# A two-layer trunk on one core: the dt product with both weight parts and both token parts side by side, the norms' first quarter added in two halves, and attention's last chunk read from its bank

## The chip, the cores and the metric

One core of a Trainium2 chip runs the kernel in one launch. The metric is the device time of an execution in microseconds (us), as the median of several. TensorE (PE in the profile) multiplies; its weight loads are listed apart (PEld). VectorE is DVE, ScalarE is ACT, GpSimd is POOL, SyncE is SP. Each engine runs its instructions in the order in which they stand in its program, and an instruction that waits holds up all that stand behind it on the same engine.

## The reference

256 tokens of 2048 columns pass two layers. Layer 0 has a Mamba-2 mixer, layer 1 has differential attention, and each is followed by a SwiGLU network of width 5632. Every one of the four sub-layers stands between two norms, and all is float32:

```python
for i in range(DEPTH):                      # DEPTH = 2
    h = rmsnorm(x, norm_mix_pre[i])
    m = ssd_mixer(h, ...) if i % 2 == 0 else diff_attention(h, ...)
    x = x + rmsnorm(m, norm_mix_post[i])
    h = rmsnorm(x, norm_ffn_pre[i])
    x = x + rmsnorm(swiglu(h, w_gate, w_up, w_down), norm_ffn_post[i])

# in the mixer: one product u @ w_in gives z, x, B, C and dt (64 columns, one for each head)
dt = softplus(dt + dt_bias);  a = -exp(a_log)
y = ssd_chunked_scan(xs * dt[..., None], dt * a, bm, cm)
```

## The kernel before

**Products.** A float32 product is made of three products of a shorter format (fp32r): weights and tokens are each cut into a high part and the rest (`hi`, `lo`), and TensorE adds hi·hi, hi·lo and lo·hi into one PSUM bank. For the weights `prep` (L126) does it, 512 columns at a time: ACT casts `hi` (L133), DVE subtracts it from the raw tile for `lo` (L134). The tokens lie in four tiles `xT[n]` of shape [128, 4, 2, 256]: for each of 16 blocks of the 2048 columns the high and the low part of all 256 tokens side by side. In the usual product (`mv`, L177) a 128-token block stands still and 512 weight columns move.

**Order.** Blocks of weights are counted by `tick`, and `later(k, fn)` (L155) hangs a piece of work k blocks further on. From this the framework's scheduler writes each engine's order when the program is built. PSUM has 8 banks: 4 for accumulators (`acc`) and 4 for all else (`aux`).

**dt.** The mixer begins with the first z chunk (`z_chunk(0)`), of weight blocks numbered hi0/lo0, hi1/lo1 and so on. Hung into it are the load of dt's 2048x64 weights, their split (`dt_split`, L366: one cast, one subtraction), and `dt_product` (L371): for each of 16 blocks three matmuls, in which the 64 weight columns stand still and 256 tokens move, 48 in all, into 64 partitions of the bank `pdt`. The tokens are not normalised yet. Their row norms come from ACT squares of the rows (`row_stats`, L381), and are spread over all partitions by two matmuls into `pb` (L312) and a DVE copy to `rstd_bc` (L313). `dt_chain` (L416) multiplies `pdt` with it and goes on in some 30 small DVE and ACT instructions on 64 partitions (softplus, the cumulated decay), which the scheduler puts between the subtractions of lo8 to lo16. `dt_token` (L446) transposes the results (`pdt_tok`).

**Norms.** The last product of each sub-layer (`out_proj`, L682) comes in four column chunks n of 512 and two token blocks t. Where a chunk's accumulator is ready, `evac` (L745) moves it to `m[(t, n)]`. For attention, where the product is made in one pass (`first`), that is an ACT copy (L749); for the others DVE adds it to what is there (L751). `sums` (L687) takes the sum of squares on ACT (L302) and multiplies by the norm's weight: POOL for n < 3, DVE into `mw` for n = 3 (L691). After the last chunk `norm_chain` (L645) runs for that t: the mean (`ms_post`, DVE, L90), its power -1/2 (`rs_post`, POOL, L93), four DVE instructions of 512 columns `x = m * rs + x` (L655), and for each of them four 128x128 transposes on TensorE into `ptx` (L661), from which ACT and DVE write the new `xT` (L666, L667). The next sub-layer's weights are then multiplied with these. The chain runs four times: step 0 behind the mixer (about 695 us), step 1 behind the first SwiGLU (1403), step 2 behind attention (1811) and, in a form that ends in the output, at the end. Last blocks of the old product (`ah_`, `al_` are the two parts of its tokens) lie beside the chain of t = 0, first blocks of the next one beside that of t = 1.

Of the kernel before, what the change touches and what calls it, by code (L numbers as in the profile page):

```python
# [16 lines left out]
P = 128  # L17
S = 256
# [23 lines left out]
def trunk_kernel(ctx, tc, x_rows, x_cols, vec_cols, vec64, post_rows, lam_rows,  # L42
# [19 lines left out]
    def aux(name):  # L62
        return auxp.tile([P, 512], F32, tag="aux", name=name)
# [300 lines left out]
        nc.sync.dma_start(dts["raw"], w_dt)  # L364

    def dt_split():  # L366
        dts["hi"] = hlA.tile([P, KD, NH], F32R, tag="hi", name="dthi")
        dts["lo"] = hlA.tile([P, KD, NH], F32R, tag="lo", name="dtlo")
        split(dts["hi"], dts["lo"], dts["raw"])

    def dt_product():  # L371
        pdt = dts["p"] = accp.tile([P, 512], F32, tag="acc", name="pdt")
        for kt in range(KD):
            xh, xl = xT_hi[kt // 4][:, kt % 4], xT_lo[kt // 4][:, kt % 4]
            for q, (w, xx) in enumerate(((dts["hi"], xh), (dts["hi"], xl), (dts["lo"], xh))):
                nc.tensor.matmul(pdt[:NH, :S], w[:, kt], xx, start=(kt == 0 and q == 0),
                                 stop=(kt == KD - 1 and q == 2))

    rs0, rh0 = [], []

# [264 lines left out]
    def norm_chain(t, ss4, last_mw, step, final, t512):  # L645

        rn = rstd_of(ss4[:, 3:4], D, f"post{step}_{t}", ss4[:, 0:1])
        for n in range(4):
            mw = last_mw if n == 3 else m[(t, n)]
            xt = xres[(t, n)]  # L650
            if final and n == 0:
                nc.scalar.activation(mw, mw, AF.Copy, scale=rn)
                nc.gpsimd.tensor_tensor(xt, xt, mw, op=ALU.add)
            else:
                nc.vector.scalar_tensor_tensor(xt, mw, rn, xt, op0=ALU.mult, op1=ALU.add)  # L655
            if final:
                nc.sync.dma_start(out[t * P:(t + 1) * P, n * 512:(n + 1) * 512], xt)
                continue
            pt = aux("ptx")
            for j in range(4):  # L660
                nc.tensor.transpose(pt[:, j * P:(j + 1) * P], xt[:, j * P:(j + 1) * P], ident)  # L661
            for j in range(4):
                sl = slice(t * P, (t + 1) * P)
                sc = pre_cols[step + 1][:, 4 * n + j:4 * n + j + 1]
                pj = pt[:, j * P:(j + 1) * P]
                nc.scalar.activation(xT_hi[n][:, j, sl], pj, AF.Copy, scale=sc)  # L666
                nc.vector.scalar_tensor_tensor(xT_lo[n][:, j, sl], pj, sc, xT_hi[n][:, j, sl].bitcast(F32),  # L667
                                               op0=ALU.mult, op1=ALU.subtract)

        def stats():  # L670
            st = small.tile([P, 4], F32, tag="ss4", name="ss_x", bufs=3)
            for n in range(4):
                row_sumsq(st[:, n:n + 1], xres[(t, n)], t512("junk"))
            s1_ = small.tile([P, 1], F32, tag="ss1", name="ssx", bufs=3)
            nc.vector.tensor_reduce(s1_, st, axis=AX.X, op=ALU.add)
            rstd[(step, t)] = rstd_of(s1_, D, f"pre{step}_{t}")


        if not final:
            later(5, stats)  # L680

    def out_proj(w, first, last, acts, kgs, step, final, lag, t512, pw, scale=None, ns=range(4), two={}, forms=None, md=None, mid=None):  # L682
# [1 line left out]

        def sums(t, n):  # L687
            mt = m[(t, n)]
            row_sumsq(ss4[t][:, n:n + 1], mt, t512("junk"))
            dst = t512("mw") if n == 3 else mt  # L690
            (nc.vector if n == 3 else nc.gpsimd).tensor_tensor(dst, mt, pw(n), op=ALU.mult)  # L691
            return dst
# [7 lines left out]
        def up_stat(i, j, t):  # L700
            return stat(up[i], j, t)

        def row(t, e):
            if t not in ss4:
                ss4[t] = small.tile([P, 4], F32, tag="ss4", name="ss_m", bufs=3)
            if e not in summed[t]:
                summed[t].add(e)
                return sums(t, e)

        ss4 = {}  # L710
        summed = {t: set() for t in range(NT)}
# [25 lines left out]
        for n in ns:  # L737
# [7 lines left out]
            def evac(t, ps, n=n):  # L745
                if first:
                    if n == 0:
                        m_tile(t)
                    nc.scalar.copy(m[(t, n)], ps)  # L749
                else:  # L750
                    nc.vector.tensor_tensor(m[(t, n)], m[(t, n)], ps, op=ALU.add)  # L751
                if not last:
                    return
                for e in range(n):
                    row(t, e)
                dst = row(t, n)
                if n == 2:
                    p3 = small.tile([P, 1], F32, tag="ss1", name="p3", bufs=3)
                    nc.vector.tensor_reduce(p3, ss4[t][:, 0:3], axis=AX.X, op=ALU.add)
                    nc.vector.tensor_scalar(ss4[t][:, 0:1], p3, 1.0 / D, EPS, op0=ALU.mult, op1=ALU.add)  # L760
                if n == 3:
                    norm_chain(t, ss4[t], dst, step, final, t512)
# [5 lines left out]
    for half in range(2):  # L768
        if half == 0:
# [2 lines left out]
            later(5, lambda: (row_stats(1), dt_split()))  # L772
            later(7, halve)
            later(8, dt_product)
            later(8, lambda: later(1, make_rstd_bc(rstd_bc, rs0, lambda: s1.tile([P, P], F32, tag="dg", name="dg"))))
            later(10, dt_chain)
            later(15, dt_token)
# [359 lines left out]
```

## Time and profile before

| | |
|---|---|
| runs | 2540.88, 2540.77, 2540.26 us; median 2540.77 |
| profiled execution | 2539.5 us, of which the span of the profile 2537.7 |
| TensorE clock granted, mean | 0.998 of full speed |
| busy: PE, DVE, ACT, POOL | 2517.8, 1902.6, 1364.7, 222.4 us |
| the chain that ended last | PE 93%, DVE 2%, ACT, issue and DMA 1% each |
| DMA | 536 MB, 211 GB/s on average |

A row of the timeline gives its start, its length, engine, line, operation, what it writes and reads, shape, and how many instructions of one kind it stands for. In brackets is how long the engine had been idle before it, and what it waited for last. Matmuls are pipelined: one of 512 columns is shown with 0.39 us, and the next starts 0.23 us after it.

### The profile page before, as it was taken

Reading aid. Unit: us, or ns where it says so; the run is one execution under the profiler, and the core shown is the slowest. Engines: PE = TensorE matmul, PEld = TensorE weight load, DVE = VectorE, ACT = ScalarE, POOL = GpSimd, SP = SyncE. Lnnn points to the kernel's source line nnn. Section 1 sums busy time; section 2 is a strip of 40 time slices with the busy share of each in tenths; the row PEclk is TensorE's granted clock in tenths of the full one; section 3 lists DMA queues with packets and bytes.
Section 4 is the critical chain, followed back from the end, with each engine's and each line's share of the span. In section 5 each row is a group of like instructions: output and inputs, shape, how many; then the busy total and the mean of one; then the engine's idle time right before and its main releaser. Section 6 shows DMA issues by size and latency. Waiting matters only on the chain.

```text
span 2537.7 us, 31211 instructions
## 1 busy us (share of the span) xinstructions
PE 2517.8 (99%) x11866; PEld 2072.2 (82%) x11866; DVE 1902.6 (75%) x2274; ACT 1364.7 (54%) x1655; POOL 222.4 (9%) x214
## 2 busy tenths in 40 slices
PE   9999999999999999999999999999999999999998
PEld 8877888788888888888888888887888888888886
DVE  6777547777687888977887765566688889878985
ACT  5767556666565454544454654455655454535453
POOL 0111000110110000001001100001100000010002
PEclk9999999999999999999999999999999999999999
DMA  7555555455776776778677544544666966786673
GB/s 287 190 169 182 189 191 198 166 183 177 254 260 210 253 238 210 236 231 243 210 237 246 189 150 166 183 151 156 241 223 201 294 216 208 235 262 213 205 252 146
DMA packets 141366, 536.16 MB, mean 211 GB/s; under 512 B 14176, under 2 KB 30880, under 8 KB 114208
## 3 DMA queue, kind: packets, MB, share of 16 engines
q1 hardware_dynamic: 125584, 502.91, 57.3%
q0 software_dynamic: 15264, 30.94, 6.5%
q8 instruction: 93, 1.52, 0.2%
q14 instruction: 57, 0.47, 0.0%
q10 hardware_dynamic: 368, 0.32, 0.0%
HBM read 516.22 MB, written 17.89 MB: 210 GB/s over the span
## 4 chain that ended last, share of the span: by engine, by line
PE 93%; DVE 2%; ACT 1%; issue 1%; DMA 1%; POOL 0%; SPq 0%; DVEq 0%; ACTq 0%; POOLq 0%
PE acc L238 38%; PE acc L187 34%; PE cp L238 8%; PE acc L212 5%; PE acc L214 2%; DVE lo L134 1%; PE sc L1013 1%; DMA mt<-acum_d 1%; PE pt_f L291 1%; ACT hi L133 1%; PE py L568 1%; PE ptx L661 0%; PE po L1049 0%; PE pc L475 0%; PE pp L1040 0%
## 5 line engine op out<-in xcount | busy, mean ns | idle before, releaser
L134 DVE TENSOR_TENSOR lo<-raw,hi 128x2048 fp32r<-128x2048 f32 (+2 forms) x451 | 848.6, 1888 | 362.4 <-ACT hi L133 353.2
L133 ACT CAST hi<-raw 128x2048 fp32r<-128x2048 f32 (+2 forms) x451 | 699.8, 1557 | 593.9 <-DVE raw L263 195.4
L238 PE MATMUL acc<-hi,xT 128*128 128x512 f32 x1840 | 589.2, 390 | 0.0
L187 PE MATMUL acc<-hi,xT 128*128 128x512 f32 x1792 | 588.9, 399 | 0.0
L238 PEld LDWEIGHTS acc<-hi,xT 128*128 128x128 f32 x1840 | 345.3, 188 | 71.5
L187 PEld LDWEIGHTS acc<-hi,xT 128*128 128x128 f32 x1792 | 335.9, 188 | 73.4 <-issue 4.9
L238 PE MATMUL acc<-lo,xT 128*128 128x512 f32 x920 | 358.1, 389 | 0.0
L187 PE MATMUL acc<-lo,xT 128*128 128x512 f32 x896 | 352.1, 393 | 1.1 <-DVE lo L134 1.1
L133 ACT CAST hi<-rawm 128x2048 fp32r<-128x2048 f32 (+1 forms) x115 | 207.8, 1807 | 173.4 <-DVE rawm L263 108.3
L134 DVE TENSOR_TENSOR lo<-rawm,hi 128x2048 fp32r<-128x2048 f32 (+1 forms) x115 | 248.0, 2157 | 69.9 <-ACT hi L133 66.1
L238 PEld LDWEIGHTS acc<-lo,xT 128*128 128x128 f32 x920 | 172.7, 188 | 35.5
L187 PEld LDWEIGHTS acc<-lo,xT 128*128 128x128 f32 x896 | 169.0, 189 | 38.0 <-DVE lo L134 3.6
L238 PE MATMUL acc<-hi,ah_f 128*128 128x512 f32 x468 | 183.1, 391 | 0.0
L238 PE MATMUL acc<-hi,al_f 128*128 128x512 f32 x468 | 182.1, 389 | 0.0
L238 PE MATMUL acc<-lo,ah_f 128*128 128x512 f32 x468 | 182.1, 389 | 0.0
L212 PE MATMUL acc<-xT,hi 128*128 128x512 f32 x512 | 179.8, 397 | 0.0
L238 PE MATMUL cp<-hi,ff 128*128 128x512 f32 x468 | 156.9, 389 | 0.0
L214 PE MATMUL acc<-xT,lo 128*128 128x256 f32 x512 | 142.6, 280 | 0.0
L138 DVE SCALAR_TENSOR_TENSOR lo<-raw,cols,hi 128x512 fp32r<-128x512 f32 x128 | 92.5, 767 | 57.2 <-ACT hi L137 56.9
L137 ACT ACTIVATE hi<-raw,cols 128x512 fp32r<-128x512 f32 x128 | 84.8, 715 | 58.9 <-PE acc L187 41.4
L212 PEld LDWEIGHTS acc<-xT,hi 128*128 128x128 f32 x512 | 96.1, 188 | 22.6
L238 PEld LDWEIGHTS acc<-hi,al_f 128*128 128x128 f32 x468 | 87.8, 188 | 18.4
(279 smaller groups left out, 3470.4 us busy)
## 6 DMA issues: line engine op xcount, KB each, us to landing
raw<-in_w_zxbc_dram SPq DMA_DIRECT2D x77, 1024.0 KB, 4.8
raw<-in_w_d_dram SPq DMA_DIRECT2D x98, 512.0 KB, 5.9
raw<-in_w_g_dram SPq DMA_DIRECT2D x96, 512.0 KB, 5.9
raw<-in_w_u_dram SPq DMA_DIRECT2D x96, 512.0 KB, 5.8
raw<-in_w_qkv_dram SPq DMA_DIRECT2D x48, 1024.0 KB, 4.8
raw<-in_w_so_dram SPq DMA_DIRECT2D x32, 1024.0 KB, 4.8
rawm<-in_w_g_dram SPq DMA_DIRECT2D x64, 512.0 KB, 5.8
rawm<-in_w_u_dram SPq DMA_DIRECT2D x64, 512.0 KB, 6.0
```

The costliest lines, as they stand in the source:

```text
L133: nc.scalar.copy(hi, raw)
L134: nc.vector.tensor_tensor(lo, raw, hi.bitcast(F32), op=ALU.subtract)
L137: nc.scalar.activation(hi[:, j], raw[:, j], AF.Copy, scale=scale[j])
L138: nc.vector.scalar_tensor_tensor(lo[:, j], raw[:, j], scale[j], hi[:, j].bitcast(F32), op0=ALU.mult, op1=ALU.subtract)
L187: nc.tensor.matmul(acc[t], a, b[:, j], start=(i == 0 and j == 0 and q == 0), stop=(i == last and j == 1 and q == 2))
L212: nc.tensor.matmul(acc[ct], hi[:, j, cs], x.rearrange("p a s -> p (a s)"), start=(i == 0 and j == 0), stop=False)
L214: nc.tensor.matmul(acc[ct][:, :S], lo[:, j, cs], x[:, 0], start=False, stop=(i == last and j == 1))
L238: nc.tensor.matmul(acc[k], a, b, start=first and q == 0, stop=last and q == 2)
L291: nc.tensor.transpose(pt[:, j], src[:, j * P:(j + 1) * P], ident)
L568: nc.tensor.matmul(py[e * 64:(e + 1) * 64, a], xd[c][:, 2 * a + e], mts[c][:, 2 * a + e], start=True, stop=True)
L1013: nc.tensor.matmul(sc[c][:, h], qT[cp, h % 2, ts], kT[cp, h % 2, :nk * P], start=True, stop=True)
```

## The change

Three places change.

- **dt.** The weights' two parts are written side by side, in two tiles of 8 blocks each, so that one stationary tile holds 64 high and 64 low columns; the 512 moving columns are the 256 high and 256 low token parts. 16 matmuls replace 48. The bank then holds four sums: high weights in partitions 0 to 63, low ones in 64 to 127, each for high and low tokens. `dt_sum` adds them: ACT copies the low tokens' half from the bank (`dta`), DVE adds the high tokens' half (`dtb`), and a matmul with a 128x64 matrix of two stacked identities (`fold`) adds the two halves of the partitions into `pdt2`. low·low is now part of the sum.
- **Norms.** The first of the four additions `x = m * rs + x` is made in two pieces of 256 columns (in the chains of steps 0, 1 and 2).
- **Attention's last chunk.** The fourth chunk isn't copied to `m`: ACT's squares and DVE's product with the norm's weight both read the accumulator's bank.

```diff
     def dt_split():
-        dts["hi"] = hlA.tile([P, KD, NH], F32R, tag="hi", name="dthi")
-        dts["lo"] = hlA.tile([P, KD, NH], F32R, tag="lo", name="dtlo")
-        split(dts["hi"], dts["lo"], dts["raw"])
+        for k in range(2):
+            d = dts[k] = hlA.tile([P, 8, 2, NH], F32R, tag=("hi", "lo")[k], name="dthl")
+            split(d[:, :, 0], d[:, :, 1], dts["raw"][:, 8 * k:8 * k + 8])
 
     def dt_product():
         pdt = dts["p"] = accp.tile([P, 512], F32, tag="acc", name="pdt")
         for kt in range(KD):
-            xh, xl = xT_hi[kt // 4][:, kt % 4], xT_lo[kt // 4][:, kt % 4]
-            for q, (w, xx) in enumerate(((dts["hi"], xh), (dts["hi"], xl), (dts["lo"], xh))):
-                nc.tensor.matmul(pdt[:NH, :S], w[:, kt], xx, start=(kt == 0 and q == 0),
-                                 stop=(kt == KD - 1 and q == 2))
+            nc.tensor.matmul(pdt, dts[kt // 8][:, kt % 8].rearrange("p a h -> p (a h)"),
+                             xT[kt // 4][:, kt % 4].rearrange("p a s -> p (a s)"),
+                             start=kt == 0, stop=kt == KD - 1)
+
+    def dt_sum():
+        a = s1.tile([P, S], F32, tag="v", name="dta", bufs=2)
+        b = s1.tile([P, S], F32, tag="th", name="dtb", bufs=2)
+        nc.scalar.copy(a, dts["p"][:, S:])
+        nc.vector.tensor_tensor(b, dts["p"][:, :S], a, op=ALU.add)
+        fold = s1.tile([P, NH], F32, tag="fold", name="fold", bufs=1)
+        nc.vector.tensor_tensor(fold, ident[:, :NH], ident[:, NH:], op=ALU.add)
+        dts["p"] = aux("pdt2")
+        nc.tensor.matmul(dts["p"][:NH, :S], fold, b, start=True, stop=True)
...
-                nc.vector.scalar_tensor_tensor(xt, mw, rn, xt, op0=ALU.mult, op1=ALU.add)
+                for sl in (slice(0, 256), slice(256, 512)) if n == 0 else (slice(0, 512),):
+                    nc.vector.scalar_tensor_tensor(xt[:, sl], mw[:, sl], rn, xt[:, sl], op0=ALU.mult, op1=ALU.add)
...
-        def sums(t, n):
-            mt = m[(t, n)]
+        def sums(t, n, mt):
...
-                return sums(t, e)
+                return sums(t, e, m[(t, e)] if mt is None else mt)
...
-                    nc.scalar.copy(m[(t, n)], ps)
+                    if not last or n < 3:
+                        nc.scalar.copy(m[(t, n)], ps)
...
-                dst = row(t, n)
+                dst = row(t, n, ps if first and n == 3 else None)
...
             later(8, dt_product)
+            later(9, dt_sum)
```

With other work to place, the scheduler also moves instructions that the diff doesn't name, at the two ends of the engines' programs that follow. Numbers behind a name are those of its buffer, and lines below L369 have another number in the new program (L417 became L429, L655 became L669, L661 became L675).

On TensorE at the end of dt's product, before: `pdt` is dt's bank, `pb` the one with the spread norms, `acc` belongs to the first z chunk.

```order
L376 MATMUL pdt_357<-xT3_102,dthi_285 64x256 x2
L376 MATMUL pdt_357<-xT3_102,dtlo_286 64x256
L312 MATMUL pb_433<-dg_406,ones_103 128x128
L312 MATMUL pb_433<-dg_407,ones_103 128x128
L187 MATMUL acc_171<-hi6_311,xT3_102 128x512
L187 MATMUL acc_196<-hi6_311,xT3_102 128x512
L187 MATMUL acc_171<-lo6_312,xT3_102 128x512
```

The same place after the change:

```order
L376 MATMUL pdt_359<-xT3_102,dthl_288 128x512 x4
L389 MATMUL pdt2_409<-dtb_404,fold_407 64x256
L312 MATMUL pb_411<-dg_376,ones_103 128x128
L312 MATMUL pb_411<-dg_377,ones_103 128x128
L187 MATMUL acc_171<-hi6_313,xT3_102 128x512
L187 MATMUL acc_196<-hi6_313,xT3_102 128x512
L187 MATMUL acc_171<-lo6_314,xT3_102 128x512
```

The `fold` matmul now stands directly behind the product whose sums ACT and DVE have to read before it, and ahead of `pb` and of all of hi6.

On DVE at the same place, before: `lo6` to `lo9` are weight subtractions, `rh0_1` is the last small step of the row norms.

```order
L391 TENSOR_SCALAR rh0_1_283<-rs_in1_281 128x1
L134 TENSOR_TENSOR lo6_312<-raw_309,hi6_311 128x1024
L134 TENSOR_TENSOR lo7_334<-raw_309,hi7_333 128x1024
L313 COPY rstd_bc_105<-pb_433 128x256
L417 TENSOR_TENSOR dtr_163<-pdt_357,rstd_bc_105 64x256
L134 TENSOR_TENSOR lo8_413<-raw_410,hi8_412 128x1024
L134 TENSOR_TENSOR lo9_438<-raw_410,hi9_437 128x1024
```

And after the change:

```order
L403 TENSOR_SCALAR rh0_1_283<-rs_in1_281 128x1
L385 TENSOR_TENSOR dtb_404<-pdt_359,dta_403 128x256
L313 COPY rstd_bc_105<-pb_411 128x256
L134 TENSOR_TENSOR lo6_314<-raw_311,hi6_313 128x1024
L134 TENSOR_TENSOR lo7_336<-raw_311,hi7_335 128x1024
L429 TENSOR_TENSOR dtr_163<-pdt2_409,rstd_bc_105 64x256
L430 TENSOR_SCALAR dtr_163<-dtr_163,v64_157 64x256
L432 SCALAR_TENSOR_TENSOR ta_164<-dtr_163 64x256
L134 TENSOR_TENSOR lo8_383<-raw_380,hi8_382 128x1024
```

The copy of `pb` has moved ahead of lo6 and lo7, behind the new `dtb`; three steps of dt's chain have moved ahead of lo8.

On DVE in the second norm chain behind attention (step 2, t = 1), before: `lo449` and `lo450` belong to the second SwiGLU's gate weights, `ms_post2_1` and `rs_post2_1` are this chain's.

```order
L134 TENSOR_TENSOR lo449_14687<-raw_14684,hi449_14686 128x2048 [waits DMAHW2_49,PE_49]
L691 TENSOR_TENSOR mw_14607<-m_14123,wpost_14359 128x512 [waits Activation_49]
L134 TENSOR_TENSOR lo450_14718<-raw_14715,hi450_14717 128x2048 [waits DMAHW3_49,PE_49,Activation_49]
L90 TENSOR_SCALAR ms_post2_1_14609<-ss_m_14125 128x1 [waits Activation_49]
L655 SCALAR_TENSOR_TENSOR x_11014<-m_14123,rs_post2_1_14611,x_11014 128x512 [waits Pool_49]
```

And after the change:

```order
L704 TENSOR_TENSOR mw_14588<-acc_14411,wpost_14341 128x512 [waits Activation_49]
L90 TENSOR_SCALAR ms_post2_1_14590<-ss_m_14107 128x1
L669 SCALAR_TENSOR_TENSOR x_10994<-m_14105,rs_post2_1_14592,x_10994 128x256 [waits Pool_49]
L669 SCALAR_TENSOR_TENSOR x_10994<-m_14105,rs_post2_1_14592,x_10994 128x256
L669 SCALAR_TENSOR_TENSOR x_10994<-m_14105,rs_post2_1_14592,x_10994 128x512
L669 SCALAR_TENSOR_TENSOR x_10996<-m_14105,rs_post2_1_14592,x_10996 128x512
L681 SCALAR_TENSOR_TENSOR xT0_99<-ptx_14596,cols_91,xT0_99 128x128 [waits Activation_49]
L669 SCALAR_TENSOR_TENSOR x_10996<-m_14105,rs_post2_1_14592,x_10996 128x512 [waits DVE_49]
L134 TENSOR_TENSOR lo450_14700<-raw_14697,hi450_14699 128x2048 [waits DMAHW3_49]
```

lo450 has gone from ahead of the chain to behind all of its additions, and `mw`, which reads the bank, waits for ACT. On TensorE, just ahead of this, the last matmul of attention's product (`acc` from hi446 and `al_o3`) stood directly behind its fellows, ahead of the 11 matmuls with hi448 and lo448; it now stands behind these 11.

## Rows read from the trace of the kernel before

**Rows 1.** The page, part 1: busy us, share, instructions of each engine.
```profile
PE 2517.8 (99%) x11866; PEld 2072.2 (82%) x11866; DVE 1902.6 (75%) x2274; ACT 1364.7 (54%) x1655; POOL 222.4 (9%) x214
```

**Rows 2.** The waits of TensorE: total us, times, longest us.
```profile
PE ptx L661 <- DVE x L655: 1.5, 3, 0.7
PE acc L187 <- DVE lo L134: 1.1, 4, 0.3
```

**Rows 3.** Line L376, dt's matmuls with the high weights: ns, first and last start.
```profile
L376 PE MATMUL pdt<-xT,dthi x32: 276/276/281, 21.8 to 29.8; 128*64 128x256 f32 x32
```

**Rows 4.** Timeline of the end of dt's product, 26 to 32 us: start, length.
```profile
26.67 0.39 PE L376 MATMUL pdt<-xT,dthi 128*64 128x256 f32 x2
...
28.02 2.00 ACT L133 CAST hi<-raw 128x1024 fp32r<-128x1024 f32 x2 [0.62 <-DMA raw<-in_w_zxbc_dram]
...
29.10 2.36 DVE L134 TENSOR_TENSOR lo<-raw,hi 128x1024 fp32r<-128x1024 f32 x2 [0.68 <-ACT hi L133]
...
29.96 0.28 PE L376 MATMUL pdt<-xT,dtlo 128*64 128x256 f32 x1
...
30.08 0.60 PE L312 MATMUL pb<-dg,ones 128*128 128x128 f32 x4
...
30.44 0.70 PE L187 MATMUL acc<-hi,xT 128*128 128x512 f32 x2
...
30.98 0.39 PE L187 MATMUL acc<-lo,xT 128*128 128x512 f32 x1
...
31.21 0.62 PE L187 MATMUL acc<-hi,xT 128*128 128x512 f32 x2
...
31.38 0.42 DVE L313 COPY rstd_bc<-pb 128x256 f32<-128x256 f32 x1
```

**Rows 5.** Windows: PE, PEld, DVE, ACT, POOL busy (instructions), granted clock, DMA.
```profile
44.00:57.00 13.00, 12.86 (x57) 9.68 (x55) 12.37 (x25) 5.55 (x8) 0.00 (x0) 1.00 0.65 230
...
136.00:140.00 4.00, 2.86 (x16) 2.52 (x17) 1.91 (x3) 2.97 (x5) 0.00 (x0) 1.00 0.54 227
```

**Rows 6.** Timeline of step 0's chains (t = 0 at 696, t = 1 at 710).
```profile
696.75 2.08 DVE L655 SCALAR_TENSOR_TENSOR x<-m,rs_post,x 128x512 f32<-128x512 f32 x3 [0.66 <-POOL rs_post L93]
...
709.81 0.50 PE L187 MATMUL acc<-lo,xT 128*128 128x512 f32 x1 [0.27 <-DVE lo L134]
...
710.39 2.28 DVE L134 TENSOR_TENSOR lo<-raw,hi 128x2048 fp32r<-128x2048 f32 x1
...
710.55 2.53 POOL L93 TENSOR_TENSOR rs_post<-ms_post,mhalf 128x1 f32<-128x1 f32 x1 [13.84 <-DVE ms_post L90]
...
713.92 0.66 PE L661 MATMUL ptx<-ident,x 128*128 128x128 f32 x4 [0.23 <-DVE x L655]
```

**Rows 7.** Timeline of step 1's second chain.
```profile
1416.12 2.29 DVE L134 TENSOR_TENSOR lo<-raw,hi 128x2048 fp32r<-128x2048 f32 x1
...
1418.46 0.50 PE L187 MATMUL acc<-lo,xT 128*128 128x512 f32 x1 [0.27 <-DVE lo L134]
```

**Rows 8.** Timeline of step 2's chains (t = 0 at 1811, t = 1 at 1823).
```profile
1811.15 0.59 ACT L749 COPY m<-acc 128x512 f32<-128x512 f32 x1 [2.17 <-PE acc L187]
...
1811.77 0.64 ACT L302 ACTIVATE junk<-m 128x512 f32<-128x512 f32 x1
1811.77 0.69 DVE L691 TENSOR_TENSOR mw<-m,wpost 128x512 f32<-128x512 f32 x1 [0.46 <-ACT m L749]
...
1814.30 0.63 PE L661 MATMUL ptx<-ident,x 128*128 128x128 f32 x4 [0.69 <-DVE x L655]
...
1823.41 0.39 PE L187 MATMUL acc<-hi,al_o 128*128 128x512 f32 x1
...
1824.32 1.92 ACT L133 CAST hi<-raw 128x2048 fp32r<-128x2048 f32 x1
...
1826.27 2.29 DVE L134 TENSOR_TENSOR lo<-raw,hi 128x2048 fp32r<-128x2048 f32 x1
...
1830.16 0.66 PE L661 MATMUL ptx<-ident,x 128*128 128x128 f32 x4
```

More of the change, by code (lines that the diff above doesn't have):

```diff
@@ L701, in up_stat, with row @@
             return stat(up[i], j, t)
-        def row(t, e):
+        def row(t, e, mt=None):
             if t not in ss4:
```

## The prediction, made before the run

> **What bounds the kernel now.** First the page: TensorE is busy for 2517.8 of the 2537.7 us [rows 1], so time can only go where its work becomes less or where it waits. Then its waits, which the reader is to compare with the three edits: at the norms it waits 1.5 us in three places for the first addition `x`, and 1.1 us in four places for a weight subtraction `lo` [rows 2]. Then the timeline at each edited place, for what stands ahead of and behind the wait on ACT and DVE [rows 4, 6 to 8]. A change under 0.2% (5.1 us) can't be told from none with this kernel; the waits that the edits can remove are below that from the start, and what remains is to see which way the small terms add up.
>
> **dt's product.** Removed are 48 matmuls. Two stand in 0.39 us where one is shown with 0.276 [rows 3, 4], so one starts 0.114 us after the other: 48 x 0.114 = 5.45 us. Added are 16 of 512 columns. Such a matmul is followed by the next after 0.23 us (30.98 and 31.21 [rows 4]): 16 x 0.23 = 3.68. The `fold` matmul is plain float32 with 256 moving columns; the nearest row is `pb`, where 0.36 us pass for 4 records of 128 columns [rows 4], so 0.36 for it. In TensorE's work this is 3.68 + 0.36 - 5.45 = -1.4 us.
>
> But the fold stands directly behind the product, with two readers of the bank between them. Before, `pb` started at 30.08; without the fold it would start 1.77 earlier, at 28.31, and the last product matmul would be done about 28.45. ACT's copy of 256 columns I price by DVE's copy of the same shape, 0.42 [rows 4], so 28.5 to 28.9; `dtb` as much, to 29.4; the fold starts about 29.45. TensorE idles for 1.1 us, `pb` follows at 29.8, hi6 at 30.2. So far 0.25 us are left of the gain (30.44 before [rows 4]). ACT casts hi6 only behind the copy, 28.9 to 29.9, in time for that.
>
> Next is DVE. Before, lo6 started at 29.10, and `rstd_bc` stood behind lo7 [rows 4]. Now `dtb` and `rstd_bc` stand ahead of lo6, and `rstd_bc` waits for `pb`: 30.4 to 30.8. lo6 runs from 30.85 for 1.18 (half of the pair's 2.36) to 32.05. The matmul that waits for it stood at 30.98 and comes 1.07 later, with 1.4 us of new idle time ahead of it. Here the saving is gone and TensorE is late.
>
> What of it remains is set some 25 us later, where TensorE transposes the ends of dt's chain. DVE, which makes this chain between its subtractions, has little slack: it is busy for 12.37 of 13.00 us from 44 to 57 us [rows 5]. It lost 1.33 us (lo6 from 29.10 to 30.85, less the 0.42 of `rstd_bc` that it has now done), and 0.63 of slack can take that up, so the chain ends about 0.6 late, and TensorE with it, whatever it saved in matmuls. **Term: +0.6**, from -1.4 (DVE has more slack before 44 than I think and the waits vanish) to +1.1. The split in two pieces casts as many columns, and its first piece is ready sooner; I cost it at nothing, since dt's first product matmuls have z matmuls beside them; without that cover the start of one more instruction on each engine, about 0.1.
>
> **The halved addition.** An addition of 512 columns takes 0.69 (2.08 for three [rows 6]); one of 256 I take at 0.42, by the nearest row of that width (`rstd_bc` [rows 4]). The first two transposes may start some 0.3 earlier; the second half has to be ready behind two transposes and a matmul, and is. In the chains of t = 0 TensorE waits 0.7 for this (1814.30 [rows 8], longest in [rows 2]). But in the new order one matmul that stood ahead of the transposes now stands behind the first two, so that TensorE comes 0.23 earlier to the wait: of 0.3 about 0.1 is gained. Three chains: **-0.2** (0 to -0.9).
>
> Its chains of t = 1 depend on what DVE does between. Step 0: the wait for a `lo` at 709.81, and the power `rs_post` at 710.55, which took 2.53 us beside the subtraction at 710.39 [rows 6], where DVE waits only 0.66 for it at 696.75 [rows 6]. The new order puts that subtraction ahead of the mean, and nothing but the additions behind it: one wait on `lo` goes (0.4 by starts), a smaller one on the next comes (0.3), five matmuls more lie ahead of the transposes at 713.92, whose wait of 0.4 by starts goes on paper. **-0.5** (-0.8 to +0.3). Step 1: the subtraction that started at 1416.12, on which the matmul at 1418.46 already waited [rows 7], now stands behind two small DVE steps which need ACT, and ACT is then loading a function table. It comes about 0.8 later and its successor 0.5, against 0.7 of waits that go: **+0.6** (-0.5 to +1.3).
>
> **The bank read directly.** It removes ACT's copy, 0.59, from the chain [rows 8]. In its place, the squares (0.64, with their sum read out some 0.8) begin at the copy's time. Before, `mw` (0.69) ran beside the squares, both at 1811.77 [rows 8]; now both read one bank, and DVE's instruction waits for ACT's. So the mean is ready after 0.8 + 0.7 instead of 0.6 + 0.8: at t = 0 it is no earlier than before (+0.1), **0**, with -0.6 as the far end.
>
> The Trainium skill, "PSUM — Partial Sum Buffer", section "PSUM bank collisions raise a hardware error", says that two engines may not be in one bank at the same time, two reads included, so that software has to order them. No row of before has two readers at once, and the new program holds the wait. If that rule and the wait were not there, both of step 2's chains would gain about 0.6, and the time would come to 2541.9 in place of the forecast.
>
> At t = 1 the order moved more. The last matmul into the bank stood at 1823.41 [rows 8], and now stands 11 matmuls later: 1823.41 + 11 x 0.23 = 1825.9, ready at 1826.3. From there: squares to 1827.15, `mw` to 1827.9, mean to 1828.1, power 0.6 to 1828.7, half an addition to 1829.1, transposes at 1829.2. They stood at 1830.16 [rows 8], but with the matmuls that TensorE has meanwhile: after the moved one 10 stand ahead of them, so it is free at 1828.4 and waits 0.8, where it had waited 0.2. ACT's cast of hi450 started at 1824.32 [rows 8] and is now behind the squares, 1827.2 to 1829.1. lo450, at 1826.27 before [rows 8], stands behind all additions: 1831.6 to 1833.9. TensorE comes to it at about 1832.7: 1.2 of new wait. **+1.8** (-0.1 to +2.5; below zero if the squares' bank is ready earlier than I count).
>
> Queues: on SP a few weight loads changed places, and on POOL one power with an accumulating DMA; the weights are two loads ahead there, which hides it. Behind 1836 us nothing moves. No instruction is cut or added elsewhere.
>
> **Sum.** 0.6 - 0.2 - 0.5 + 0.6 + 0 + 1.8 = +2.3 us. The profiled execution took 2539.5 (span 2537.7 and 1.8 around it), the median of the runs is 1.3 above it: 2539.5 + 2.3 + 1.3 = 2543.1, so **2543 us**, within 0.2% of before.
>
> **Rivals.**
> 1. *The removed work pays.* dt's -1.4 stays because DVE catches up before TensorE transposes the chain; halves and bank read gain their far ends at t = 0, and t = 1 costs nothing. For it: all the waits named are DVE's or ACT's, and before 44 us ACT waits often. Against: DVE at 12.37 of 13.00 [rows 5]. -1.4 - 0.9 - 0.5 - 0.6 = -3.4: 2537.4 us. Even this is within 0.2%.
> 2. *lo450 holds up what stands behind it* (the slower side). Its 2.29 us [rows 8] now lie on DVE between the additions and the subtractions that make the next tokens' low parts. If TensorE needs these as soon as lo450, it waits the 2.29 once more on top of the 1.2, and step 2 costs 4.1 in place of 1.8. It decides from the point where TensorE's first matmul with the new low parts stands less than 2.3 us behind its first with lo450. For it: the additions of t = 1 end at 1831.6, one subtraction behind another. Against: the weights of hi449 to hi451 with t = 0 are work that TensorE still has. 2545.4 us; with dt's upper end as well 2545.9, with step 1's 2546.6.
> 3. *A lowered clock.* The two new pauses of 1.1 and 1.4 lie within 4 us. Were the granted clock to fall from 2.4 to 1.2 GHz for those 4 us, they would take 4 us more: 2547 us. Against: behind the longest wait of the kernel, in the stretch from 136 to 140 where TensorE is busy for 2.86 of 4.00, it stands at 1.00 [rows 5].
> 4. *Nothing moves:* the scheduler's changes and the edits cancel at each place, 2540 to 2541 us. For it: the sum's terms are each smaller than their ranges.
>
> **Chances.** Forecast (2541.5 to 2544.5) 0.47; rival 4 0.2; rival 1 0.17; rival 2 0.12; rival 3 0.04. The range of 8 in 10 leaves out rival 3, the last part of rival 2 and the lower part of rival 1: 2537.5 to 2546. Faster by over 0.2% would be below 2535.7, beyond even rival 1, and is left for what I overlook: 0.06. Slower by over 0.2% is above 2545.9: rival 3, half of rival 2 and a little of the forecast's upper end, 0.12. The same: 0.82.
>
> **What would show it.** On the page after: TensorE's instructions fall, its busy time hardly. dt right: a matmul of line 389 starts about 1.1 us after the product, a matmul with lo6 waits about 1.4 us for DVE, and the first matmuls of hi16 stand 0.3 to 0.9 later than before; wrong, if hi16 is earlier than before. The bank read right: `mw` starts when the squares end, 0.8 after them, at both t; wrong, if they overlap. Step 2 right: a matmul waits some 1.2 us for lo450; wrong, if lo450 is there in time. The halves: transposes of two, not four, ahead of the next matmul, the wait ahead of them 0.1 shorter at t = 0. The whole is wrong if TensorE's waits in the three chains together fall by more than 1 us, or if a place that I hold for unmoved, behind 1836 us, differs.

## The result, and the profile after

The changed kernel takes 2544.31 us (median of 22 executions, 2542.29 to 2545.37), the kernel before beside it 2539.91 (22, 2539.15 to 2541.11): 4.4 us more, ratio 1.0016 with a 95% interval of 1.0010 to 1.0023. The profiled execution took 2543.73 us, of which the span 2542.0.

TensorE's work hardly changed on the page (2517.8 us in [rows 1]), so the loss is waits:

```profile
PE 2517.2 (99%) x11836; PEld 2070.8 (81%) x11836; DVE 1904.8 (75%) x2283; ACT 1363.5 (54%) x1655; POOL 219.7 (9%) x214
```

The waits of TensorE after the change (total us, times, longest), to be laid beside [rows 2]:

```profile
PE acc L187 <- DVE lo L134: 3.8, 4, 1.2
PE ptx L675 <- DVE x L669: 2.1, 5, 0.6
...
PE pdt L389 <- DVE dtb L385: 0.9, 1, 0.9
...
PE cp L238 <- DVE lo L134: 0.3, 1, 0.3
PE py L580 <- ACT mt L523: 0.2, 1, 0.2
```

The wait for a weight subtraction `lo` has risen from 1.1 to 3.8 us in as many places, and the one for the new `dtb` is added; the two small ones at the end are not among the waits of before. Where they came is read by following one matmul through both traces: counted in order on its line, the same matmul starts so much later after the change:

| landmark (time before) | later by, us | what lies between |
|---|---|---|
| 20 us | 0.15 | start |
| 31.4, dt's end | 1.49 | fold and lo6 |
| 62 | 1.24 | dt's chain |
| 690 | 1.61 | no edited place |
| 709 | 1.42 | step 0, t = 0 |
| 735 | 1.00 | step 0, t = 1 |
| 1395 | 1.31 | no edited place |
| 1436 | 2.17 | step 1 |
| 1812 | 2.82 | no edited place |
| 1822 | 2.51 | step 2, t = 0 |
| 1838 | 4.24 | step 2, t = 1 |
| 2525 | 4.23 | no edited place |

So dt costs about 1.2 (0.15 of it from the start on), step 0 gives 0.6, step 1 costs 0.9, step 2 gives 0.3 and then costs 1.7: 2.9 us at the edited places. The other 1.3 are hops, places between the edited ones at which the lateness grows by up to 0.3 us. Two of them, 0.30 at 124 us and 0.24 at 1018, are the two small waits above. The experiments show what the hops are worth.

**dt.** The timeline of the changed kernel from 28 to 33 us, the counterpart of [rows 4]:

```profile
28.55 0.37 ACT L384 COPY dta<-pdt 128x256 f32<-128x256 f32 x1 [0.71 <-PE pdt L376]
...
28.82 3.98 ACT L133 CAST hi<-raw 128x1024 fp32r<-128x1024 f32 x4
28.95 0.43 DVE L385 TENSOR_TENSOR dtb<-pdt,dta 128x256 f32<-128x256 f32 x1
29.43 0.65 PE L389 MATMUL pdt<-dtb,fold 128*64 128x256 f32 x2 [0.92 <-DVE dtb L385]
...
30.47 0.71 PE L187 MATMUL acc<-hi,xT 128*128 128x512 f32 x2
30.76 0.42 DVE L313 COPY rstd_bc<-pb 128x256 f32<-128x256 f32 x1 [1.38 <-PE pb L312]
31.10 2.35 DVE L134 TENSOR_TENSOR lo<-raw,hi 128x1024 fp32r<-128x1024 f32 x2
32.37 0.50 PE L187 MATMUL acc<-lo,xT 128*128 128x512 f32 x1 [1.18 <-DVE lo L134]
```

hi6's first matmul stands where it stood (30.47 for 30.44): what the shorter product saved went into the wait for the fold. DVE sat idle for 1.38 us until `pb` was there, then copied it, and only then made lo6, whose matmul comes at 32.37 in place of 30.98. Behind that TensorE gets hardly any of it back: from 44 to 57 us it was busy for 12.86 of 13.00 us before [rows 5], and is so throughout after the change (busy PE, PEld, DVE, ACT, POOL; granted clock, DMA):

```profile
44.00:57.00 13.00, 13.00 (x58) 10.24 (x57) 12.21 (x25) 5.75 (x7) 0.00 (x0) 1.00 0.73 244
```

**Norms.** Step 0's second chain, the counterpart of [rows 6]:

```profile
711.40 2.28 DVE L134 TENSOR_TENSOR lo<-raw,hi 128x2048 fp32r<-128x2048 f32 x1
...
714.49 0.55 POOL L93 TENSOR_TENSOR rs_post<-ms_post,mhalf 128x1 f32<-128x1 f32 x1 [16.17 <-DVE ms_post L90]
...
715.61 0.44 PE L675 MATMUL ptx<-ident,x 128*128 128x128 f32 x2 [0.22 <-DVE x L669]
```

The power takes 0.55 where it took 2.53, as no subtraction lies beside it now. In step 1 the subtraction on which [rows 7] already waited comes later:

```profile
1418.29 2.29 DVE L134 TENSOR_TENSOR lo<-raw,hi 128x2048 fp32r<-128x2048 f32 x1
...
1420.62 0.50 PE L187 MATMUL acc<-lo,xT 128*128 128x512 f32 x1 [1.06 <-DVE lo L134]
```

It started at 1416.12 before; of the 2.17 between, 1.37 are the lateness that TensorE already had, 0.80 are new.

**Step 2**, both chains, the counterpart of [rows 8]:

```profile
1813.97 0.60 ACT L302 ACTIVATE junk<-acc 128x512 f32<-128x512 f32 x1 [2.17 <-PE acc L187]
...
1814.69 0.69 DVE L704 TENSOR_TENSOR mw<-acc,wpost 128x512 f32<-128x512 f32 x1 [0.56 <-ACT junk L302]
...
1816.80 0.41 PE L675 MATMUL ptx<-ident,x 128*128 128x128 f32 x2 [0.59 <-DVE x L669]
...
1828.41 0.39 PE L187 MATMUL acc<-hi,al_o 128*128 128x512 f32 x1
...
1828.84 0.60 ACT L302 ACTIVATE junk<-acc 128x512 f32<-128x512 f32 x1 [2.48 <-PE acc L187]
...
1829.42 1.90 ACT L133 CAST hi<-raw 128x2048 fp32r<-128x2048 f32 x1
...
1829.56 0.69 DVE L704 TENSOR_TENSOR mw<-acc,wpost 128x512 f32<-128x512 f32 x1 [1.13 <-ACT junk L302]
...
1831.58 0.44 PE L675 MATMUL ptx<-ident,x 128*128 128x128 f32 x2 [0.51 <-DVE x L669]
...
1834.08 2.28 DVE L134 TENSOR_TENSOR lo<-raw,hi 128x2048 fp32r<-128x2048 f32 x1
...
1836.42 0.50 PE L187 MATMUL acc<-lo,xT 128*128 128x512 f32 x1 [1.00 <-DVE lo L134]
```

The squares begin where the copy began (1811.15 + 2.82), `mw` begins 0.72 after them, where both began together before. At t = 1 the last al_o matmul stands at 1828.41 (1823.41 before: 2.5 by the lateness, 2.5 by the 11 matmuls), and lo450 is ready 1.0 us after TensorE wants it.

### The profile page after: what moved, and what is told of

Same layout as the page of the kernel before. It is cut to its first block, busy times and chain, and to the rows that moved or that the text cites. A ratio compares the mean times of both kernels' runs of the same rounds, so it can differ in the third digit from the quotient of the medians.

```text
span 2542.0 us, 31156 instructions
## 1 busy us (share of the span) xinstructions
PE 2517.2 (99%) x11836; PEld 2070.8 (81%) x11836; DVE 1904.8 (75%) x2283; ACT 1363.5 (54%) x1655; POOL 219.7 (9%) x214
## 4 chain that ended last, share of the span: by engine, by line
PE 93%; DVE 2%; ACT 2%; issue 1%; DMA 1%; POOL 0%; SPq 0%; DVEq 0%; ACTq 0%; POOLq 0%
PE acc L238 38%; PE acc L187 34%; PE cp L238 8%; PE acc L212 5%; PE acc L214 2%; DVE lo L134 1%; PE sc L1028 1%; ACT hi L133 1%; DMA mt<-acum_d 1%; PE pt_f L291 1%; PE py L580 1%; ACT mt L523 0%; PE po L1064 0%; PE ptx L675 0%; PE pc L487 0%
```

## The experiments

Each was timed beside the kernel before on the same chip, over 11 executions, the last two kernels over one each. The median of before was 2540.28 us for the first four and for the next four, 2540.73 for the two after. The difference given behind each time is the one to that median. Besides, the same matmul is followed through the traces as above.

**dt's part alone** (the hunks of `dt_split`, `dt_product` and `dt_sum`):

```diff
...
+            later(9, dt_sum)
```

> Only the dt part of the change; norms and attention's last chunk as before. Theory: DVE, with dtb and the copy of pb ahead of lo6, and TensorE behind the fold make dt's part about +1.3 us late at lo6 and +1.1 at the first matmuls of hi16, and nothing after that differs: +1.1 us against before in the whole. Rival: the small shifts that the changed kernel's trace shows behind dt (+0.25 near 150 us, +0.3 near 1018, +0.65 between 1490 and 1690) come from the changed order and belong to this part: then this kernel shows them too and the whole is +2 or more.

2543.08 us, +2.8, ratio 1.0010 (1.0001 to 1.0019). In its trace dt costs 1.2 at 62 us, and nothing moves at the norms; hops of 0.2 to 0.3 follow at 124, 152, 1018 and near 1630. The place is as expected, the median is 1.7 us above it. Neither theory is met as a whole, and the rival is met in part: the hops at 124 (0.29 to 0.32) and at 1018 (0.24 to 0.31) stand in all four traces of kernels with dt's part as in the change. In the nine others the first is 0.15 at most and the second absent, so these two go with dt's part and its order; why, is open. Hops at the other places stand in kernels without dt's part too.

**The halved addition alone:**

```diff
+                for sl in (slice(0, 256), slice(256, 512)) if n == 0 else (slice(0, 512),):
```

> Only the halved first addition. My account in the prediction put the loss behind attention (t = 1) down to the bank read. Theory now: it is the halves that make the scheduler put the last al_o matmul 11 matmuls later, and that alone costs the chain. In this kernel lo450 stays ahead of the mean on DVE, behind a cast of hi450 that waits for the late copy: TensorE waits about 2.2 us for lo450, and step 2 is +2.0 in all; step 0 -0.6, step 1 +0.85, so +2.2 us against before. Rival (the bank read is what costs): step 2 here gains 0.3 at t = 0 and loses nothing at t = 1, and the whole is about 0 (-0.6 + 0.85 - 0.3).

2544.50, +4.2, ratio 1.0016 (1.0007 to 1.0025): as much as the whole change. In the trace step 0 -0.66, step 1 +0.85, step 2 -0.24 at t = 0 and +3.98 at t = 1. The rival, which was the account of the prediction, falls: the loss behind attention is there without the bank read. It is larger than expected (3.7 in step 2 for 2.0), though the wait for lo450 is shorter (1.83 for 2.2); the reason is in the clock. Its timeline and a window behind that wait:

```profile
1832.52 0.50 PE L187 MATMUL acc<-lo,xT 128*128 128x512 f32 x1 [1.83 <-DVE lo L134]
```

```profile
1834.00:1836.00 2.00, 2.00 (x9) 1.51 (x8) 2.00 (x5) 0.37 (x1) 0.00 (x0) 0.58 0.86 356
```

The clock granted from 1834 to 1838 is 0.57 to 0.58: TensorE has fallen mostly to 1.2 GHz after the pause. The 4 us at that clock are worth about 1.7 us, nearly as much as the pause itself (an estimate: 4 us times the missing 0.43).

**The bank read alone:**

```diff
-                    nc.scalar.copy(m[(t, n)], ps)
+                    if not last or n < 3:
+                        nc.scalar.copy(m[(t, n)], ps)
-                dst = row(t, n)
+                dst = row(t, n, ps if first and n == 3 else None)
```

> Only the last chunk read from its bank. Theory: the last al_o matmul stays where it was, mw waits for the squares, so t = 0 is the same within 0.1; at t = 1 the mean comes ahead of lo450, the power then runs beside lo450 and takes some 2.5 us instead of 0.55, the transposes stand where they stood: 0 in the whole (-0.3 to +0.3). Rival (the bank read costs): +1.4 to +1.8 at t = 1 as in the changed kernel. Second rival (the copy's 0.59 is gained at both t): -0.6 to -1.2.

2540.66, +0.4, ratio 1.0002 (0.9993 to 1.0011). In the trace step 2 is -0.1 at t = 0 and 0.0 at t = 1. Theory right in each step; the timeline of t = 1 has the power beside lo450:

```profile
1826.16 0.69 DVE L690 TENSOR_TENSOR mw<-acc,wpost 128x512 f32<-128x512 f32 x1
...
1826.95 2.29 DVE L134 TENSOR_TENSOR lo<-raw,hi 128x2048 fp32r<-128x2048 f32 x1
1827.05 2.61 POOL L93 TENSOR_TENSOR rs_post<-ms_post,mhalf 128x1 f32<-128x1 f32 x1 [13.04 <-DVE ms_post L90]
```

Its trace has hops of about 0.3 too, at 1574 and 1645, where the change touches nothing: hops at these two places go with no single part of the change.

**dt's part without the sum behind it:**

```diff
-    def dt_sum():
...
-            later(9, dt_sum)
```

> The dt part alone with dt_sum left out: dt is taken from partitions 0 to 63 and the first 256 columns of the bank, so the products with a low part are missing from dt. It removes ACT's copy, dtb, the fold matmul and the wait for them. Theory A (the fold's wait is the cost): the 1.77 us of saved matmuls stay, lo6's matmul comes 1 us earlier than before and the whole is -1.0 or better. Theory B (TensorE has nothing to do at that point: hi6's weights land at 28.0, the last row norm's diagonal is ready at 29.4, and rstd_bc with three dt steps stands ahead of lo6 on DVE): TensorE waits there as long as with the fold, lo6's matmul is again over 1 us later than before, and the whole is between 0 and +1.

2543.42, +3.1, ratio 1.0012 (1.0004 to 1.0021). Theory A falls: with the copy, `dtb`, the fold and its wait gone, nothing is gained. Theory B has the mechanism, its size was too small. But the order isn't that of the changed kernel: three dt steps stand ahead of lo6 here, which stand behind lo7 there, so this loss isn't the same one. The timeline:

```profile
29.18 0.61 POOL L307 TENSOR_SCALAR dg<-ident,rs_in 128x128 f32<-128x128 f32 x1
29.84 0.49 PE L312 MATMUL pb<-dg,ones 128*128 128x128 f32 x2 [1.39 <-POOL dg L307]
...
32.00 2.35 DVE L134 TENSOR_TENSOR lo<-raw,hi 128x1024 fp32r<-128x1024 f32 x2
...
33.27 0.80 PE L187 MATMUL acc<-lo,xT 128*128 128x512 f32 x1 [2.47 <-DVE lo L134]
```

TensorE stands for the row norms' diagonal instead of the fold, and `rstd_bc` with three dt steps still delays lo6. The window behind it:

```profile
33.20:36.30 3.10, 3.04 (x7) 2.46 (x8) 3.10 (x5) 1.22 (x2) 0.00 (x0) 0.50 0.27 45
```

Here the clock is at 0.50 for 3 us; at 36 us this kernel is 3.8 us late, at 61 us 2.6.

**dt's part with `pb` copied by ACT** (against dt's part alone):

```diff
-            nc.vector.tensor_copy(dst, pb[:, :S])
+            nc.scalar.copy(dst, pb[:, :S])
```

> The dt part alone, with pb copied to rstd_bc by ACT in place of DVE; the fold and its wait stay as in the changed kernel, and on DVE lo6 and lo7 now stand directly behind dtb. Theory (what makes dt's part late is DVE's order, rstd_bc ahead of lo6): lo6 runs as soon as hi6 is cast, 29.9 to 31.1, its matmul is at most 0.2 later than before, and dt's part costs 0 (-0.3 to +0.3) where it cost +1.2. Rival (TensorE's wait for the fold is what costs, 0.9 us in the changed kernel): the wait is unchanged, so dt's part stays at +1.0 to +1.3.

2540.13, -0.15, ratio 0.9999 (0.9990 to 1.0008): against their kernels before, 2.95 us less than dt's part with DVE's copy, by one line on another engine. The line makes two copies; at the other, at 1441 us, the trace's lateness doesn't change. The theory is right by the time, not by the trace. The execution profiled was the longest of eleven (2542.47): the second load of the rows landed late, so that the square over them began at 27.27 (24.4 to 27.1 in the other traces), `dtb` stood on DVE behind the norms of these rows, and the fold waited 2.07. Behind that wait the granted clock fell, to 0.67 from 31 to 32 us and 0.50 from 32 to 34, and two matmuls of hi6 took 1.20 where they take 0.71 in the changed kernel:

```profile
27.27 1.91 ACT L302 ACTIVATE rows<-rows 128x2048 f32<-128x2048 f32 x1 [1.75 <-DMA rows<-in_x_rows_dram]
...
30.70 0.65 PE L389 MATMUL pdt<-dtb,fold 128*64 128x256 f32 x2 [2.07 <-DVE dtb L385]
30.80 2.36 DVE L134 TENSOR_TENSOR lo<-raw,hi 128x1024 fp32r<-128x1024 f32 x2 [0.16 <-ACT hi L133]
...
32.10 1.20 PE L187 MATMUL acc<-hi,xT 128*128 128x512 f32 x2
```

lo6's matmul is 2.1 later than before there and TensorE 2.7 late at 62 us, though lo6 itself no longer waits for `pb`. So in single executions a long wait for the fold does cost; the median says that it isn't the usual case.

**Halves in chosen chains** (against the halved addition alone):

```diff
-... if n == 0 else
+... if n == 0 and (step == 0 or (step == 1 and t == 1) or (step == 2 and t == 1)) else
```

> Only the halved addition, in the chains of step 0 (both t), of step 1 at t = 1 and of step 2 at t = 1; no dt part, no bank read. In this order lo385, lo450 and the last al_o matmul keep their places. Theory: step 0 gains 0.6 as in the changed kernel, the other two lose nothing (0 to -0.3 each): -0.6 to -1.0 by the trace, too little for the medians to tell from before. Rival (halving at t = 1 is what costs in steps 1 and 2): +0.8 and +1.5 or more there.

2540.22, -0.06, ratio 1.0000 (0.9991 to 1.0009). In the trace step 0 -0.62, step 1 -0.04, step 2 +0.1: the halves cost nothing where lo385, lo450 and the al_o matmul keep their places, and gain something in step 0 alone.

**Halves and bank read, without dt's part:**

```diff
+                for sl in (slice(0, 256), slice(256, 512)) if n == 0 else (slice(0, 512),):
+                dst = row(t, n, ps if first and n == 3 else None)
```

> Halves and bank read together, without the dt part. Theory: the bank read costs nothing alone, and beside the halves it takes part of their loss behind attention away, since lo450 then stands behind the additions and no longer ahead of the mean: step 0 -0.6, step 1 +0.85, step 2 +1.4 as in the changed kernel, +1.7 in all, where the halves alone had +3.7 in step 2. Rival (the halves' +3.7 in step 2 was one execution's chance, or depends on dt): +3 or more here too.

2541.72, +1.4, ratio 1.0007 (0.9998 to 1.0016). Step 0 -0.65, step 1 +0.86, step 2 +1.41, nearly as in the changed kernel. Beside the halves the bank read helps: 1.41 in step 2 of the traces against 3.74 for the halves alone, of which about 1.7 are the fallen clock there.

**In step 2 only t = 0 halved** (against the halved addition alone):

```diff
-... if n == 0 else
+... if n == 0 and (step == 0 or (step == 2 and t == 0)) else
```

> Only the halved addition, in step 0 (both t) and in step 2 at t = 0 alone; in step 2 at t = 1 the addition is whole. Theory: halving t = 0 gains 0.25 there, and by the one matmul that it puts behind the transposes makes the scheduler move the last al_o matmul of t = 1 behind 11 others; the chain of t = 1 pays for that, 3 to 4 us, though nothing is halved in it. With step 0's -0.6 the whole is +2.3 to +3.2. Rival (the loss comes from the halves of t = 1): step 2 gains 0.25, -0.85 in the whole.

2542.48, +2.2, ratio 1.0009 (1.0000 to 1.0018). Step 0 -0.62; step 2 -0.27 at t = 0, +2.44 at t = 1, where nothing is halved:

```profile
1824.83 0.39 PE L187 MATMUL acc<-hi,al_o 128*128 128x512 f32 x1
...
1827.68 2.29 DVE L134 TENSOR_TENSOR lo<-raw,hi 128x2048 fp32r<-128x2048 f32 x1 [1.11 <-ACT hi L133]
...
1830.03 0.50 PE L187 MATMUL acc<-lo,xT 128*128 128x512 f32 x1 [1.83 <-DVE lo L134]
```

The theory holds by the place: halving t = 0 moves the last al_o matmul of t = 1. Its size, 3 to 4 us, was too large for this trace. TensorE waits 1.83 us for lo450, as with all chains halved, but here the granted clock stays at 1.00 behind it (1.00 from 1830 to 1842); that is about the 1.5 us between this kernel's t = 1 and that of the halves alone. The execution profiled is the shortest of eleven (2540.89, mean granted clock 0.998). Seven of the others, of 2542.16 to 2543.10, have a mean of 0.997, so the clock may well have fallen in most of them; no trace shows it.

**The whole change with `pb` copied by ACT** (against the changed kernel):

```diff
-            nc.vector.tensor_copy(dst, pb[:, :S])
+            nc.scalar.copy(dst, pb[:, :S])
```

> The changed kernel whole, with pb copied by ACT in place of DVE, so that lo6 and lo7 stand directly behind dtb on DVE. Theory: dt's part no longer costs (it was +2.8 by the medians where it stood alone, 0 with this copy), and what is left is halves and bank read together, +1.4: 2541.7 us. Rival (the earlier zero was chance, the fold's wait costs as much as ever): 2544.3 as the changed kernel.

2542.15, +1.4, ratio 1.0006 (0.9997 to 1.0015), as expected against its own before. The trace shows how dt's loss is gone although the fold waits longer than in the changed kernel:

```profile
29.61 0.65 PE L389 MATMUL pdt<-dtb,fold 128*64 128x256 f32 x2 [1.26 <-DVE dtb L385]
29.74 2.36 DVE L134 TENSOR_TENSOR lo<-raw,hi 128x1024 fp32r<-128x1024 f32 x2 [0.18 <-ACT hi L133]
...
30.94 0.37 ACT L313 COPY rstd_bc<-pb 128x256 f32<-128x256 f32 x1 [0.28 <-PE pb L312]
31.21 0.40 PE L187 MATMUL acc<-lo,xT 128*128 128x512 f32 x1
```

lo6 runs beside the fold and `pb`, its matmul is 0.23 later than before, and at 62 us TensorE is 0.06 early.

**The parts that didn't lose, together** (against the changed kernel; the bank read is left out as well):

```diff
-            nc.vector.tensor_copy(dst, pb[:, :S])
+            nc.scalar.copy(dst, pb[:, :S])
-... if n == 0 else
+... if n == 0 and (step == 0 or (step == 1 and t == 1) or (step == 2 and t == 1)) else
```

> dt's part with pb copied by ACT, and the halves only in step 0 and, at t = 1, in steps 1 and 2; no bank read. Theory: dt 0, halves -0.6 to -0.9 by the trace: 2539.5, which the medians can hardly tell from before. In the trace the matmul with lo6 follows DVE by at most 0.2 later than before where the second row load lands by 26.0 us; rival (TensorE's wait for the fold is carried on): the first matmuls of hi16 are 0.8 us or more later than before and the whole is at 2541 or above.

2539.73 against 2540.73, ratio 0.9996 (0.9987 to 1.0005): 1.0 us below its kernel before, where the changed kernel is 4.4 above its own, but not told apart from the kernel before. In its profiled execution, the longest of eleven (2540.72), the rows landed late again (the square at 27.07) and the fold waited 1.99, here with the clock at 1.00 behind it; hi16 was 0.8 late there, which was the rival's sign, while the time is not the rival's.

**dt's part alone, two more executions:**

> The dt part alone once more, for a second profile: eleven executions of it lay between 2541.5 and 2545.3 us, and the one profiled was among the quickest. Theory (the late row load makes lo6 later in some executions, and TensorE's two pauses at 28 to 33 us are then long enough for the granted clock to fall): an execution of 2543 us or more shows lo6's matmul over 2 us late and a granted clock well under 1.00 between 33 and 37 us. Rival (the spread comes from places far from dt): lo6's matmul is 1.3 late as before and the rest of the time is lost elsewhere.

> The same kernel, for a third profile, with the same two expectations: a longer execution with a late row load, a later lo6 and a fallen clock behind it, or with the loss elsewhere.

2541.84 and 2541.23. lo6's matmul stands at 33.07 and 32.10, the fold waited 1.75 and 0.92, at 62 us they are 1.9 and 0.9 late, and the clock of the first is 1.00 throughout 28 to 40 us. In that one the rows' square began at 26.71: a late load and a lo6 2.1 late don't suffice for a long execution. Neither of the two is one of the long executions of 2543 us and more. Three profiles of this kernel show 0.9 to 1.9 us for dt's part at 62 us, 1.6 to 2.5 with the hops at 124 and 1018, where its median and that with ACT's copy differ by 2.95. The rest, 0.4 to 1.4 us, is in no trace of it. A fallen clock behind the waits, as in the kernel without the fold and with ACT's copy, would account for it. The mean granted clock of each execution speaks for that: among the eleven of dt's part alone it is 0.997 in four of the five longest (2543.20 to 2545.25) and 0.998 in the six others; without the fold it is 0.997 in seven of eleven, the profiled one with its fallen clock among them. These means are coarse, though: the profiled execution with ACT's copy has 0.998 with a fallen clock in its trace, and of the changed kernel's 22 only two have 0.997. So the account is likely, not shown.

## Why the prediction was right, and where it was not

The forecast was 2543 us within 2537.5 to 2546; it is 2544.3, slower by 0.16%, on the side and in the range foreseen, with the likeliest case. Rivals 4 and 1 are out. Rivals 2 and 3 did not occur in the profiled execution of the changed kernel; the fallen clock of rival 3 did occur at dt's place in two of the kernels made from it. That the time is within 1.3 us of the forecast is in part luck: the loss was forecast at 2.3 us and is 4.4, but the kernel before took 2539.9 beside it and not the 2540.8 from which the forecast starts. By its steps:

- *dt*: the replay was right to 0.3 us place by place (fold at 29.43 for 29.45, hi6 at 30.47 for 30.2, lo6's matmul at 32.37 for 32.05). The term, +0.6, was too small: 1.2 in the trace, 1.8 with the two hops that go with it, and near 3 by the medians. It failed at the step from DVE's slack to the end of the chain: of the lateness at lo6 only 0.25 us came back by 62 us, not half. DVE's slack (1.33 less 0.63 is 0.7, not 0.6) was the wrong thing to count, as TensorE, itself busy for 12.86 of 13.00 us there, had hardly any idle time from which to give the lateness back. By the medians the cause is not the fold's wait, which took most of the working, but `rstd_bc` ahead of lo6: the copy on ACT, with a longer wait for the fold (1.26 for 0.92), loses nothing in the whole change's trace and nothing by the medians. The kernel without the fold loses as much, but in another order.
- *Halves at t = 0*: -0.2 forecast for three chains; measured -0.2, +0.1 and -0.3 in the changed kernel.
- *Step 0, t = 1*: -0.5 forecast, -0.4 measured. *Step 1*: +0.6 forecast, +0.9 measured.
- *Bank read, t = 0*: 0 forecast; -0.1 measured alone. That `mw` would wait for the squares is in the rows: 1814.69 behind 1813.97, both at 1811.77 in [rows 8]. The Trainium skill, "PSUM — Partial Sum Buffer", section "PSUM bank collisions raise a hardware error", wants two readers of one bank kept apart; in the trace they are, at 0.72 us between the two starts, by the wait that the program holds. What they would do without it no run here shows.
- *Step 2, t = 1*: +1.8 forecast, +1.7 measured, and every instruction within 0.5 us of the forecast when the lateness of 2.5 is taken off (transposes at 1829.1 for 1829.2, lo450 at 1831.6 for 1831.6). But the step that laid this on the bank read was wrong. Halving t = 0 moves the al_o matmul; the bank read alone costs 0, and beside the halves the chain of t = 1 costs 1.7 with it, 2.4 (t = 0 halved) to 4.0 (all halved) without it, because lo450 then no longer stands ahead of the mean.
- Unforeseen: 1.3 us of hops between the edited places in the profiled execution. The two at 124 and 1018 us, 0.5 together, go with dt's part. The others stand in kernels with other edits too and are no part of any one edit. How much of the medians' 4.4 us is hops and how much is the rest of dt's near 3 us, which no trace holds, stays open.

## What to carry to other kernels

Before an edit's own saving is counted, read in the new order what now stands ahead of the next weight preparation on the engine that makes it: here one 0.42 us copy ahead of a subtraction, for whose input DVE first waits 1.38 us, cost 1.2 us and more in the trace and near 3 by the medians, and moving that copy to an engine with room gave it back. Slack on the engine that is late gives nothing back where TensorE itself is never idle. A scheduler that places instructions by its own estimate can answer an edit in one chain with a move in the next, so each part of a change is to be timed alone and in pairs; the parts here are worth +2.8, +4.2 and +0.4 alone and +4.4 together. A wait of TensorE costs more than its length where the clock falls behind it: the chain with a wait of 1.83 us for lo450 cost 4.0 us with the clock at 0.57 and 2.4 with the clock at 1.00.

## What the runs showed of the hardware

- The granted clock can fall behind a pause of under 2 us. It was 0.57 to 0.58 behind a wait of 1.83 us with half additions following, 0.50 behind a wait of 2.07 (dt's part with ACT's copy), 0.50 behind waits of 1.39 and 2.47 within 5 us, and 1.00 behind waits of 0.92 and 1.18 (the changed kernel), of 1.75 and 1.18 (dt's part again), of 1.99 (the parts together), of 1.83 (step 2 with t = 0 halved alone) and in [rows 5]. The same wait was followed by either; what decides is not shown.
- POOL's power of one column takes 0.55 to 0.57 us alone and 2.53 to 2.61 beside DVE's subtraction of 2048 columns, in four chains: the second of steps 0 and 1 before, of step 1 after, and of step 2 with the bank read alone. The Trainium skill, "SBUF — State Buffer", section "SBUF: two separate sides", gives GpSimd and a DVE instruction with two inputs in SBUF one shared pair of ports, held by one instruction at a time; the trace agrees, as the power ends 0.4 us after the subtraction each time ([rows 6]: 713.08 and 712.67).
- The landing of one load of 1 MB in the first 30 us varies between executions, and a wait that hangs on it varies with it: the square over it begins between 24.39 and 27.27 in the traces of all kernels, and at 24.58, 25.95 and 26.71 in the three of dt's part alone, where the fold waited 0.92, 1.13 and 1.75.
